# A two-layer mLSTM and band-attention trunk: pieces of x, the gates' products and their selection in the first phase

## The chip, the cores and the metric

The kernel runs on one core of a Trainium2 chip. The metric is the device time of one execution in microseconds; several executions are timed and the median is given. Engines are named as in the profile: PE (matrix products) and PEld (its weight loads), DVE (vector), ACT (scalar, with function tables), POOL, and SP, which issues most transfers.

## The reference

`x` is 512 tokens by 2048 features, batch 1, float32. Two layers follow, each with a pre-norm modulated by a conditioning vector `c`, a mixer, and a gated, normalised residual. The first layer is an mLSTM with 8 heads, the second a chunked band attention. The change touches the start of the first layer:

```python
sc = jax.nn.silu(c)
mod = sc @ ada_w[l] + ada_b[l]                 # shift, scale, gate
h = rmsnorm(x, g_pre[l]) * (1 + scale) + shift
proj = h @ w_in                                # 2048 x (2*2048 + 3*4096 + 16)
qk = silu(causal_conv(proj[..., :A_V0]))       # queries, keys
v, o, z = ...                                  # 4096 columns each
gates = proj[..., A_G0:] + gate_b              # the last 16 columns
li = gates[..., :8]                            # input gates of 8 heads
lf = log_sigmoid(gates[..., 8:])               # forget gates of 8 heads
ht = mlstm_chunkwise(q, k, v, li, lf)          # then head norm, sigmoid(o), silu(z), w_out
```

## The kernel before

Activations lie transposed: 16 depth tiles of 128 features by 512 tokens. Float32 precision is made from three products of a high and a low part (`mm3`): each weight piece is split by ACT into a high part (`wh`) and by DVE into the rest (`wl`), and so is each depth tile of the normalised input (`h1[k]`, parts 0 and 1). A product of 128 by 128 weights with 512 tokens is one PE instruction.

**The start.** SP issues the loads in a fixed order (`pin` keeps program order): `c`, then `x` in four pieces of 4 depth tiles (`xt`, L538), the column constants, small constants (`kcs`, with the identity and a selection matrix `sel`), the first adaLN rows, the first weight pieces. ACT squares a piece two tiles at a time (L583), DVE adds the squares (L586, L588), and PE sums over features for each piece (`token_sums`, tile `ps_x`), with wake-up products (`awake`, tile `ps_idle`) after each but the first. ACT takes the root (L594), DVE the reciprocal (L597), PE spreads it over partitions (`ps_rb`), and the first depth tile of the input is made (L481 to L484, tiles `h1t` and `h`).

**The first phase.** A depth tile of the input is ready only when DVE has summed its two adaLN columns, shift and scale, each a pass over 2048 values per partition (L512). So head 0's columns, and some of head 1's, are computed depth tile by depth tile. `LEAD` lists the columns whose sums stay in PSUM for the whole phase (tile `ps_lead`, five banks of pool `psP` and one of `psA`): each depth tile multiplies all of them at once. `LATER` lists the other columns. They are worked off block by block (`BLOCKS`: depth tiles 0-1, 2-5, 6-11, 12-15) while the next block's depth tiles are being prepared; each column's block sum goes through a `psA` bank (tile `ps_l`) and is copied (L683) or added by DVE (L685) into SBUF. `first_steps()` deals these steps out between the depth tiles. Weight pieces are read in the order of `stream()`, and SP's loads of adaLN rows are interleaved at fixed pieces (`fetch_first`).

**The gates.** After the phase the 2048 by 16 gate weights are loaded (`graw`, L697) and split into a high and a low part side by side (`gw`, 32 columns). In head 0 `gates()` multiplies them with both parts of all 16 depth tiles (tile `ps_g`, 32 products), copies the 32 rows to SBUF (L707), and folds them with two small products by `sel` into `ps_li` and `ps_f` (8 rows each). A chain on ACT and DVE (L714 to L732) makes the log gates, their running sums and maxima.

The scheduler orders each engine's queue by priority, which is program order unless `high_priority` raises it; a queue, once ordered, is worked off in order. PSUM has eight banks, five in `psP` and three in `psA`. `background()` fetches the remaining adaLN rows through POOL and lets DVE sum them.

Of the kernel before, what the change touches and what calls it, by code (L numbers as in the profile page):

```python
# [9 lines left out]
F32 = mybir.dt.float32  # L10
# [5 lines left out]
P = 128  # L16
D = 2048
S = 512
# [13 lines left out]
REL = 257  # L32
EXTW = 640
AHEAD = 300
RAW_BUFS = 3

PAIRS = [(0, 1), (2, 3)]
BLOCKS = [(0, 2), (2, 6), (6, 12), (12, 16)]
LEAD = [0, P, V0 // 2, V0 // 2 + P, O0, O0 + P]
LATER = [O0 + 2 * P, O0 + 3 * P] + [Z0 + i * P for i in range(4)]  # L40
LATER += [DK, DK + P, V0 // 2 + DK, V0 // 2 + DK + P]


# [19 lines left out]
def first_steps():  # L63


    out, left = [], []
    for k0, k1 in BLOCKS:
        n = k1 - k0
        for j in range(n):
            out += left[-(-len(left) * j // n) : -(-len(left) * (j + 1) // n)] + [(k0 + j,)]  # L70
        g = 2 if n <= 4 else 1
        left = [(k0, k1, i, g) for i in range(0, len(LATER), g)]
    return out + left


# [82 lines left out]
def hybrid_trunk(ctx, tc, xT, xN, c, adaT, cols, wst, wg, ext, kc, out):  # L158
# [23 lines left out]
    y2c = [dram.tile([P, 2, S], F32, name=f"y2c{i}") for i in range(BH // 2)]  # L182

    cl = const.tile([P, NCOL], F32, name="cl")
    kcs = const.tile([P, 144], F32, name="kcs")
    ones_f = const.tile([P, P], F32, name="ones_f")
    cst = const.tile([P, 4], F32, name="cst")
    mod = const.tile([P, 128], F32, name="mod")
# [7 lines left out]
    nc.vector.memset(cst[:, 1:2], 1.0)  # L196
    eps_c, one_c = cst[:, 0:1], cst[:, 1:2]
    ident = kcs[:, 0:128]
    sel = kcs[:32, 128:144]

    def col(i):
        return cl[:, i : i + 1]
# [330 lines left out]
        pin(nc.sync.dma_start(crow[i], c[i * S : (i + 1) * S].unsqueeze(0)))  # L533
    xt, xq = [], []
    rstd0 = ssum
    for q in range(4):
        t = sp.tile([P, 4, S], F32, name=f"xt{q}")
        pin(nc.sync.dma_start(t, xT[q]))  # L538
        xq.append(t)
        xt += [t[:, j, :] for j in range(4)]  # L540
        if q == 1:
            pin(nc.sync.dma_start(cl, cols))
    pin(nc.sync.dma_start(kcs, kc[:, :144]))
    early = [ada_load(KT, ap_, 2, pin, 2), ada_load(0, sp, 2, pin, 2)]
    steps = first_steps()
    coming = {}

    def fetch_first(n):

        while wpos[0] < min(n, len(steps)):  # L550
            i = wpos[0]
            raw_load(pin)
            if i == 0:
                coming[1] = ada_start(1)
            for k in range(2, KT):
                if i == steps.index((k - 2,)) + 2:
                    coming[k] = ada_start(k)

    fetch_first(3)
# [16 lines left out]

    silu_c(0)
    silu_c(1)
    for q in range(4):
        pair = []  # L580
        for i in range(2):
            sq = xp.tile([P, 2, S], F32, tag="x", name=f"xsq{q}_{i}")
            pin(nc.scalar.activation(sq, xq[q][:, 2 * i : 2 * i + 2, :], AF.Square))  # L583
            if q < 2 and i == 0:
                silu_c(2 + q)
            pin(nc.vector.tensor_tensor(sq[:, 0, :], sq[:, 0, :], sq[:, 1, :], op=ALU.add))  # L586
            pair.append(sq[:, 0, :])
        pin(nc.vector.tensor_tensor(pair[0], pair[0], pair[1], op=ALU.add))  # L588
        token_sums(pair[0], q == 0, q == 3)
        if q:  # L590
            awake(256 if q < 3 else 128)
# [12 lines left out]
    pin(nc.scalar.copy(rstd0, psr))  # L604
    ada_sum(*early[1], pin)
    h1 = []
    lead = [newp(f"ps_lead{i}") for i in range(5)] + [newa("ps_lead5")]
    oz = [acp.tile([P, S], F32, tag="so", name=f"oz0_{i}", bufs=6) for i in range(6)]
    oz += [q1p.tile([P, S], F32, tag="oz", name=f"oz0_{i}", bufs=2) for i in range(6, 8)]
    qk1 = [q1p.tile([P, S], F32, tag="q1", name=f"q1_{i}", bufs=4) for i in range(4)]  # L610
    later = oz[2:] + qk1
    split_n = [1]

    def split_first(n):
# [24 lines left out]
    def background(n):  # L639
# [4 lines left out]
        while pending and len(loaded) < 3:  # L644
            p, bufs = (bp, 1) if len(pending) % 3 == 1 else (ap_, 2)
            loaded.append(ada_load(pending.pop(0), p, bufs, pin, queue=nc.gpsimd))

    due = []
    for n, step in enumerate(steps):
        if n > len(steps) - 6:  # L650
            background(2 if n % 2 else 0)
        if n:
            split_first(n + 2)
        if due:
            column_sums(due.pop())
        if len(step) == 1:
            [k] = step
            ht = xp.tile([P, 2, S], F32R, tag="x", name=f"h1_{k}")
            tmp = tp.tile([P, S], F32, tag="t", name=f"h1t_{k}")
            *begun, done = modulated(  # L660
                xt[k], rstd0 if k else psr, amul[:, k : k + 1], mod[:, k : k + 1], ht[:, 0, :], ht[:, 1, :], tmp,
                lambda ins: ins if k else pin(ins),
            )
            if k == 0:
                first[:] = *begun, done
            h1.append(ht)
            proj("a_w_in", h1, lead, 1, k, k + 1, KT - 1, first=0)
            if k + 1 < KT:
                due.append(k + 1)
            if k == 0:  # L670
                column_sums(due.pop())
                fetch_first(4)
            continue
        k0, k1, i0, g = step
        [(hi, lo)] = wpiece("a_w_in")
        for i in range(g):
            ps, acc = newa(f"ps_l{i0 + i}_{k0}"), later[i0 + i]
            for k in range(k0, k1):
                w = slice(((k - k0) * g + i) * P, ((k - k0) * g + i + 1) * P)
                mm3(ps, hi[:, w], lo[:, w], h1[k][:, 0, :], h1[k][:, 1, :], k == k0, k == k1 - 1)  # L680
            with tc.high_priority(AHEAD if k0 else 0):
                if k0 == 0:
                    behind(nc.scalar.copy(acc, ps), parted[1])  # L683
                else:
                    nc.vector.tensor_tensor(acc, acc, ps, op=ALU.add)  # L685
# [5 lines left out]
    ones_r = hp.tile([P, P], F32R, name="ones_r")  # L691
    nc.vector.memset(ones_r.bitcast(F32), 1.0)
    maskd = hp.tile([P, P], F32, name="maskd")
    nc.sync.dma_start(maskd, kc[:, 144:272])
    graw = tp.tile([P, KT, 16], F32, tag="t", name="graw")
    gw = hp.tile([P, KT, 32], F32R, tag="p0", name="gw")
    nc.sync.dma_start(graw, wg)  # L697
    split(gw[:, :, 0:16], gw[:, :, 16:32], graw)


    def gates():
        g_ps = newa("ps_g")
        for k in range(KT):
            for i in range(2):
                mm(g_ps[:32], gw[:, k, :], h1[k][:, i, :], k == 0 and i == 0, k == KT - 1 and i == 1)
        g32 = tp.tile([P, S], F32, tag="t", name="g32")
        nc.scalar.copy(g32[:32], g_ps[:32])  # L707
        ps_i, ps_f = newa("ps_li"), newa("ps_f")
        mm(ps_i[:8], sel[:, 0:8], g32[:32], True, True)
        mm(ps_f[:8], sel[:, 8:16], g32[:32], True, True)  # L710
        f, u, w = (hp.tile([P, S], F32, tag=t, name=f"gate_{t}")[:8] for t in ("nm", "nmd", "p1"))
        e = ssum[:8]
        gbi, gbf = cl[:8, GB : GB + 1], cl[:8, GB + 1 : GB + 2]
        nc.scalar.activation(f, ps_f[:8], AF.Identity, bias=gbf)  # L714
        nc.scalar.activation(e, f, AF.Abs)
        nc.scalar.activation(e, e, AF.Exp, scale=-1.0)
        nc.vector.tensor_scalar(u, e, 1.0, None, op0=ALU.add)
        nc.vector.scalar_tensor_tensor(e, u, -1.0, e, op0=ALU.add, op1=ALU.subtract)
        nc.vector.reciprocal(w, u)
        nc.vector.tensor_tensor(e, e, w, op=ALU.mult)  # L720
        nc.scalar.activation(u, u, AF.Ln)
        nc.vector.tensor_tensor(u, u, e, op=ALU.subtract)
        nc.vector.scalar_tensor_tensor(f, f, 0.0, u, op0=ALU.min, op1=ALU.subtract)
        on = tp.tile([P, S], F32, tag="t", name="gate_one")[:8]
        nc.vector.memset(on, 1.0)
        nc.vector.tensor_tensor_scan(u, on, f, 0.0, ALU.mult, ALU.add)
        nc.vector.scalar_tensor_tensor(e, ps_i[:8], gbi, u, op0=ALU.add, op1=ALU.subtract)
        nc.vector.tensor_tensor_scan(w, e, e, 0.0, ALU.max, ALU.max)
        nc.vector.tensor_scalar(on, w, -1.0, None, op0=ALU.mult)
        nc.sync.dma_start(gsc[0], on)  # L730
        nc.vector.tensor_tensor(w, u, w, op=ALU.add)
        nc.scalar.activation(w, w, AF.Exp, scale=-1.0)  # L732
        nc.sync.dma_start(gsc[1], w)
        pt = newa("ps_at")
        for j in range(4):
            nc.tensor.transpose(pt[:, j * 8 : j * 8 + 8], e[:, j * P : (j + 1) * P], ident[:8, :8])
        nc.vector.tensor_copy(aT.rearrange("p a b -> p (a b)"), pt[:, :32])
# [88 lines left out]
    for h in range(NH):  # L826
# [24 lines left out]
        if h == 0:  # L851
            background(2)
            gates()
            for i in range(4):
                nc.scalar.activation(so[i], lead[4 + i] if i < 2 else so[i], AF.Sigmoid)
        nm = hp.tile([P, S], F32, tag="nm", name=f"nm{h}")
        em = ssum
        nmd = hp.tile([P, 4, P], F32, tag="nmd", name=f"nmd{h}")
# [566 lines left out]
def layouts(x, c, ada_w, ada_b, g_pre, g_post, a_w_in, a_conv_w, a_conv_b, a_gate_b, a_g_head,  # L1425
# [3 lines left out]
    def cc(v):  # L1429
        return np.asarray(v).reshape(-1, P).T  # L1430

    xT = np.ascontiguousarray(x[0].T.reshape(4, 4, P, S).transpose(0, 2, 1, 3))
    xN = np.ascontiguousarray(x[0].reshape(4, P, D))
    adaT = np.concatenate([ada_w[0].T, ada_w[1].T, kv_ada_w.T], 0).reshape(128, P, D)
    gb = np.zeros((P, 2), f)
# [14 lines left out]
    rel = b_rel[0]  # L1450
    u = np.clip(384 + (P - 1) - np.arange(EXTW), -128, 128) + 128
    ext = np.ascontiguousarray(rel[:, u])
    kc = np.zeros((P, 272), f)
    kc[:, :128] = np.eye(P)
    i = np.arange(P)
    kc[:32, 128:144] = np.tile(np.eye(16), (2, 1))
    kc[:, 144:272] = np.where(i[None, :] >= i[:, None], 0.0, NEG)
    return {
        "xT": xT, "xN": xN, "c": np.ascontiguousarray(c[0]), "adaT": np.ascontiguousarray(adaT), "cols": np.ascontiguousarray(cols),
        "wst": wst, "wg": wg, "ext": ext, "kc": kc,  # L1460
# [17 lines left out]
```

## Time and profile before

| | |
|---|---|
| median of 3 runs | 2753.21 us (2752.81 to 2754.87) |
| the profiled execution | 2749.57 us, span 2747.5 us |
| PE busy | 2725.0 us (99%) |
| DVE, ACT busy | 2322.9 us (85%), 1436.2 us (52%) |
| DMA | 527.26 MB, mean 192 GB/s |
| granted PE clock | 0.999 |

The span runs from the first to the last instruction; the execution's own time has 2.07 us more around it. "Idle before, releaser" in a row is the time in which the engine stood still ahead of the instruction and what ended it. Rows of a stage give busy time and, in brackets, the number of instructions that touch the stage. DVE shares its busy time unevenly: it is almost full in the first 140 us.

### The profile page before, as it was taken

The page shows a single profiled execution, that of the slowest core. Times are in us where ns is not written, and L with a number is a line of the kernel's source. Part 1 is how long each engine was busy: PE and PEld are TensorE (multiplying, and loading weights), DVE is VectorE, ACT ScalarE, POOL GpSimd, SP SyncE. Part 2 cuts the span into 40 slices and gives each one's busy share as a digit, 9 for nine tenths or more (in the row PEclk, how much of TensorE's full clock was granted, in tenths as well). Part 3 has the DMA queues.
Part 4 walks back from the last instruction along what each step waited for, and adds up shares of the span by engine and source line. Part 5 has one row for each costly group of instructions (what it writes and reads, how often), then busy time and mean ns, then how long its engine had stood idle before and what let it go on. Part 6 is the DMA issues. An engine that isn't in the chain of part 4 may idle for free.

```text
span 2747.5 us, 45189 instructions
## 1 busy us (share of the span) xinstructions
PE 2725.0 (99%) x17554; PEld 2485.9 (90%) x17554; DVE 2322.9 (85%) x3768; ACT 1436.2 (52%) x2046; POOL 30.5 (1%) x61
## 2 busy tenths in 40 slices
PE   8999999999999999999999999999999999999998
PEld 6887888899999999999998888888998999999887
DVE  8988989989999898998988677467995798899666
ACT  4243533556556555565646344568444566666523
POOL 0000010000000000000000000000000000000000
PEclk9999999999999999999999999999999999999999
DMA  9777697333333333333337788788645544444697
GB/s 368 289 263 266 253 375 291 107 99 125 108 116 109 102 125 101 116 110 101 125 101 259 260 294 306 232 282 272 214 146 192 169 123 130 127 125 126 213 305 254
DMA packets 170913, 527.26 MB, mean 192 GB/s; under 512 B 18325, under 2 KB 34229, under 8 KB 158921
## 3 DMA queue, kind: packets, MB, share of 16 engines
q1 hardware_dynamic: 162490, 464.61, 50.6%
q0 software_dynamic: 8208, 59.77, 5.7%
q8 instruction: 137, 2.24, 0.3%
q14 instruction: 78, 0.64, 0.1%
HBM read 490.69 MB, written 38.85 MB: 193 GB/s over the span
## 4 chain that ended last, share of the span: by engine, by line
PE 88%; issue 6%; DVE 3%; DMA 2%; POOL 1%; ACT 1%; SPq 0%; DVEq 0%; POOLq 0%; ACTq 0%
PE ps_y L281 19%; PE ps_azo L281 5%; PE ps_czo L281 5%; PE ps_dzo L281 5%; PE ps_kv L281 5%; PE ps_az L281 3%; PE ps_cz L281 3%; PE ps_dz L281 3%; PE ps_l L281 3%; PE ps_bzo L281 3%; PE ps_czq L281 2%; PE ps_cv L281 2%; PE ps_azq L281 2%; PE ps_dzq L281 2%; PE ps_dv L281 2%
## 5 line engine op out<-in xcount | busy, mean ns | idle before, releaser
L214 ACT CAST wh<-wr 128x1024 fp32r<-128x1024 f32 (+1 forms) x560 | 579.5, 1037 | 534.6 <-PE ps_y L281 205.7
L214 DVE TENSOR_TENSOR wl<-wr,wh 128x1024 fp32r<-128x1024 f32 (+1 forms) x560 | 672.4, 1204 | 183.7 <-ACT wh L214 182.7
L281 PE MATMUL ps_y<-wh,y 128*128 128x512 f32 x1536 | 476.2, 390 | 0.0
L214 ACT CAST wsh<-ws 128x768 fp32r<-128x768 f32 (+1 forms) x272 | 222.5, 818 | 426.8 <-issue 124.8
L281 PEld LDWEIGHTS ps_y<-wh,y 128*128 128x128 f32 x1536 | 288.2, 188 | 59.9 <-ACT sqy L1011 0.2
L214 DVE TENSOR_TENSOR wsl<-ws,wsh 128x768 fp32r<-128x768 f32 (+1 forms) x272 | 253.7, 933 | 91.6 <-ACT wsh L214 88.7
L281 PE MATMUL ps_y<-wl,y 128*128 128x512 f32 x768 | 299.1, 389 | 0.0
L512 DVE CUSTOM_DVE_ANT_0 ada<-ada,scB,cl 128x2048 f32<-128x2048 f32 (+1 forms) x89 | 205.9, 2321 | 14.1 <-DMA ada<-in_adaT 13.8
L253 DVE TENSOR_TENSOR ws<-wr 128x512 f32<-128x512 f32 (+1 forms) x272 | 181.0, 670 | 1.9 <-DMA wr<-in_wst 1.8
L281 PEld LDWEIGHTS ps_y<-wl,y 128*128 128x128 f32 x768 | 144.3, 188 | 29.9 <-DVE wl L214 0.4
L281 PE MATMUL ps_kv<-wh,hkv 128*128 128x512 f32 x512 | 159.5, 390 | 0.0
L281 PE MATMUL ps_v<-wh,h 128*128 128x512 f32 x384 | 120.3, 390 | 0.0
L281 PEld LDWEIGHTS ps_kv<-wh,hkv 128*128 128x128 f32 x512 | 96.1, 188 | 19.9
L255 DVE TENSOR_TENSOR ws<-wr 128x256 f32<-128x256 f32 (+1 forms) x272 | 110.9, 412 | 2.8
L254 DVE TENSOR_TENSOR wr<-ws,wr 128x256 f32<-128x256 f32 (+1 forms) x272 | 110.4, 411 | 1.9
L281 PE MATMUL ps_kv<-wl,hkv 128*128 128x512 f32 x256 | 100.0, 391 | 0.8 <-DVE wl L214 0.8
L281 PE MATMUL ps_l<-h,wh 128*128 128x512 f32 x320 | 98.5, 390 | 0.0
L281 PEld LDWEIGHTS ps_v<-wh,h 128*128 128x128 f32 x384 | 71.9, 188 | 14.7
L281 PE MATMUL ps_azo<-h,wh 128*128 128x256 f32 (+1 forms) x404 | 82.1, 294 | 0.0
L281 PE MATMUL ps_v<-wl,h 128*128 128x512 f32 x192 | 74.9, 390 | 0.0
L281 PEld LDWEIGHTS ps_l<-h,wh 128*128 128x128 f32 x320 | 59.9, 188 | 12.8 <-ACT wh L214 0.3
L281 PE MATMUL ps_dzo<-h,wh 128*128 128x256 f32 x364 | 69.6, 283 | 0.0
(443 smaller groups left out, 7231.8 us busy)
## 6 DMA issues: line engine op xcount, KB each, us to landing
wr<-in_wst SPq DMA_DIRECT2D x530, 512.0 KB, 4.0
ada<-in_adaT POOLq DMA_DIRECT2D x57, 1024.0 KB, 7.0
ada<-in_adaT SPq DMA_DIRECT2D x30, 1024.0 KB, 8.1
adq<-in_adaT SPq DMA_DIRECT2D x92, 256.0 KB, 4.5
ada<-in_adaT SPq DMA_DIRECT2D x36, 512.0 KB, 5.7
xt<-nsc SPq DMA_DIRECT2D x48, 256.0 KB, 3.6
wr<-in_wst SPq DMA_DIRECT2D x26, 384.0 KB, 8.0
yr<-ysc SPq DMA_DIRECT2D x28, 256.0 KB, 5.5
```

Source lines behind the costliest of these rows:

```text
L214: ins = nc.scalar.copy(hi, src), nc.vector.tensor_tensor(lo, src, hi.bitcast(F32), op=ALU.subtract)
L253: nc.vector.tensor_tensor(t[:, : 2 * w], r[:, w : 3 * w], r[:, : 2 * w], op=ALU.subtract)
L254: nc.vector.tensor_tensor(r[:, w : 2 * w], t[:, w : 2 * w], r[:, :w], op=ALU.add)
L255: nc.vector.tensor_tensor(t[:, 2 * w :], r[:, 3 * w :], r[:, w : 2 * w], op=ALU.subtract)
L281: product[0] = nc.tensor.matmul(ps, a, b, start=start, stop=stop)
L512: pin(nc.vector.tensor_tensor_reduce(c, c, (sc or scB)[:, j * w : (j + 1) * w], 1.0, mod[:, i : i + 1] if j else col(CB + i), ALU.mult, AL ...
```

## The change

Three edits. `x` comes in pieces of 4, 4, 6 and 2 depth tiles instead of four of 4; the squares' adds follow the size of the piece. The sixth lead column tile moves to the later ones (five lead, eleven later), and its `psA` bank is taken by the gates' sum: the gate weights are loaded early, split when depth tile 2 is ready, and each depth tile's two gate products are issued right behind its lead products (depth tiles 0 and 1 together with 2). The two selecting products become one, whose 40 rows hold the input gates at 0 to 7 and the forget gates at 32 to 39.

```diff
+CHUNKS = [4, 4, 6, 2]
-LEAD = [0, P, V0 // 2, V0 // 2 + P, O0, O0 + P]
-LATER = [O0 + 2 * P, O0 + 3 * P] + [Z0 + i * P for i in range(4)]
+LEAD = [0, P, V0 // 2, V0 // 2 + P, O0]
+LATER = [O0 + i * P for i in range(1, 4)] + [Z0 + i * P for i in range(4)]
 LATER += [DK, DK + P, V0 // 2 + DK, V0 // 2 + DK + P]
@@ first_steps
-        left = [(k0, k1, i, g) for i in range(0, len(LATER), g)]
+        left = [(k0, k1, i, min(g, len(LATER) - i)) for i in range(0, len(LATER), g)]
@@ loads
-    for q in range(4):
-        t = sp.tile([P, 4, S], F32, name=f"xt{q}")
-        pin(nc.sync.dma_start(t, xT[q]))
+    for q, n in enumerate(CHUNKS):
+        t = sp.tile([P, n, S], F32, name=f"xt{q}")
+        pin(nc.sync.dma_start(t, xT[P * len(xt) : P * (len(xt) + n)].rearrange("(p j) t -> p j t", j=n)))
...
+    graw = sp.tile([P, KT, 16], F32, name="graw")
+    gw = sp.tile([P, KT, 32], F32R, name="gw")
@@ fetch_first
                 if i == steps.index((k - 2,)) + 2:
+                    if k == 2:
+                        pin(nc.sync.dma_start(graw, wg))
                     coming[k] = ada_start(k)
@@ squares
-    for q in range(4):
+    for q, n in enumerate(CHUNKS):
         pair = []
-        for i in range(2):
+        for i in range(n // 2):
...
-        pin(nc.vector.tensor_tensor(pair[0], pair[0], pair[1], op=ALU.add))
+            if i:
+                pin(nc.vector.tensor_tensor(pair[0], pair[0], pair[i], op=ALU.add))
@@ first phase
-    lead = [newp(f"ps_lead{i}") for i in range(5)] + [newa("ps_lead5")]
+    lead = [newp(f"ps_lead{i}") for i in range(5)]
+    g_ps = newa("ps_g")
...
-    later = oz[2:] + qk1
+    later = oz[1:] + qk1
...
+    gated = []
+
+    def gate_products():
+
+        while len(gated) < len(h1):
+            k = len(gated)
+            for i in range(2):
+                mm(g_ps[:32], gw[:, k, :], h1[k][:, i, :], k == 0 and i == 0, k == KT - 1 and i == 1)
+            gated.append(k)
...
             proj("a_w_in", h1, lead, 1, k, k + 1, KT - 1, first=0)
+            if k == 2:
+                split(gw[:, :, 0:16], gw[:, :, 16:32], graw, done, begun[1])
+            if k > 1:
+                gate_products()
@@ gates
-        g_ps = newa("ps_g")
-        for k in range(KT):
-            for i in range(2):
-                mm(g_ps[:32], gw[:, k, :], h1[k][:, i, :], k == 0 and i == 0, k == KT - 1 and i == 1)
         g32 = tp.tile([P, S], F32, tag="t", name="g32")
         nc.scalar.copy(g32[:32], g_ps[:32])
-        ps_i, ps_f = newa("ps_li"), newa("ps_f")
-        mm(ps_i[:8], sel[:, 0:8], g32[:32], True, True)
-        mm(ps_f[:8], sel[:, 8:16], g32[:32], True, True)
+        ps = newa("ps_if")
+        mm(ps[:40], sel, g32[:32], True, True)
...
-        nc.scalar.activation(f, ps_f[:8], AF.Identity, bias=gbf)
+        nc.scalar.activation(f, ps[32:40], AF.Identity, bias=gbf)
...
-        nc.vector.scalar_tensor_tensor(e, ps_i[:8], gbi, u, op0=ALU.add, op1=ALU.subtract)
+        nc.vector.scalar_tensor_tensor(e, ps[:8], gbi, u, op0=ALU.add, op1=ALU.subtract)
@@ head 0
-                nc.scalar.activation(so[i], lead[4 + i] if i < 2 else so[i], AF.Sigmoid)
+                nc.scalar.activation(so[i], so[i] if i else lead[4], AF.Sigmoid)
```

The host's layout of `x` and of the small constants follows.

More of the change, by code (lines that the diff above doesn't have):

```diff
@@ L184, in hybrid_trunk @@
     cl = const.tile([P, NCOL], F32, name="cl")
-    kcs = const.tile([P, 144], F32, name="kcs")
+    kcs = const.tile([P, 168], F32, name="kcs")
     ones_f = const.tile([P, P], F32, name="ones_f")
@@ L198, in hybrid_trunk @@
     ident = kcs[:, 0:128]
-    sel = kcs[:32, 128:144]
+    sel = kcs[:32, 128:168]
     def col(i):
@@ L535, in hybrid_trunk @@
     rstd0 = ssum
-    for q in range(4):
-        t = sp.tile([P, 4, S], F32, name=f"xt{q}")
-        pin(nc.sync.dma_start(t, xT[q]))
+    for q, n in enumerate(CHUNKS):
+        t = sp.tile([P, n, S], F32, name=f"xt{q}")
+        pin(nc.sync.dma_start(t, xT[P * len(xt) : P * (len(xt) + n)].rearrange("(p j) t -> p j t", j=n)))
         xq.append(t)
-        xt += [t[:, j, :] for j in range(4)]
+        xt += [t[:, j, :] for j in range(n)]
         if q == 1:
             pin(nc.sync.dma_start(cl, cols))
-    pin(nc.sync.dma_start(kcs, kc[:, :144]))
+    pin(nc.sync.dma_start(kcs, kc[:, :168]))
     early = [ada_load(KT, ap_, 2, pin, 2), ada_load(0, sp, 2, pin, 2)]
+    graw = sp.tile([P, KT, 16], F32, name="graw")
+    gw = sp.tile([P, KT, 32], F32R, name="gw")
     steps = first_steps()
@@ L693, in hybrid_trunk @@
     maskd = hp.tile([P, P], F32, name="maskd")
[L694 to L698, printed above, removed]
+    nc.sync.dma_start(maskd, kc[:, 168:296])
     def gates():
-        g_ps = newa("ps_g")
-        for k in range(KT):
-            for i in range(2):
-                mm(g_ps[:32], gw[:, k, :], h1[k][:, i, :], k == 0 and i == 0, k == KT - 1 and i == 1)
         g32 = tp.tile([P, S], F32, tag="t", name="g32")
         nc.scalar.copy(g32[:32], g_ps[:32])
-        ps_i, ps_f = newa("ps_li"), newa("ps_f")
-        mm(ps_i[:8], sel[:, 0:8], g32[:32], True, True)
-        mm(ps_f[:8], sel[:, 8:16], g32[:32], True, True)
+        ps = newa("ps_if")
+        mm(ps[:40], sel, g32[:32], True, True)
         f, u, w = (hp.tile([P, S], F32, tag=t, name=f"gate_{t}")[:8] for t in ("nm", "nmd", "p1"))
@@ L1430, in cc @@
         return np.asarray(v).reshape(-1, P).T
-    xT = np.ascontiguousarray(x[0].T.reshape(4, 4, P, S).transpose(0, 2, 1, 3))
+    xT = x[0].T.reshape(KT, P, S)
+    ends = np.cumsum([0] + CHUNKS)
+    xT = np.concatenate([xT[a:b].transpose(1, 0, 2).reshape(-1, S) for a, b in zip(ends, ends[1:])])
     xN = np.ascontiguousarray(x[0].reshape(4, P, D))
@@ L1452, in layouts @@
     ext = np.ascontiguousarray(rel[:, u])
-    kc = np.zeros((P, 272), f)
+    kc = np.zeros((P, 296), f)
     kc[:, :128] = np.eye(P)
     i = np.arange(P)
-    kc[:32, 128:144] = np.tile(np.eye(16), (2, 1))
-    kc[:, 144:272] = np.where(i[None, :] >= i[:, None], 0.0, NEG)
+    kc[:32, 128:136], kc[:32, 160:168] = np.split(np.tile(np.eye(16), (2, 1)), 2, 1)
+    kc[:, 168:296] = np.where(i[None, :] >= i[:, None], 0.0, NEG)
     return {
```

## The prediction

> **What bounds the kernel now.** I read the page first, then the matrix engine's waits in the first 210 us, then the busy time of the stages around them, then the start instruction by instruction. The page gives the engines' shares of the 2747.5 us span.
>
> ```profile
> PE 2725.0 (99%) x17554; PEld 2485.9 (90%) x17554; DVE 2322.9 (85%) x3768; ACT 1436.2 (52%) x2046; POOL 30.5 (1%) x61
> ```
>
> PE is nearly always busy, so an edit can win only where PE waits or does needless work. The changed code lies in the first 240 us. PE's waits there, between the first lead product and the end of the first phase, with total, times and longest, are four groups:
>
> ```profile
> PE ps_lead L281 <- ACT h L483: 2.3, 3, 1.5
> PE ps_l L281 <- DVE wl L214: 0.9, 2, 0.6
> PE ps_lead L281 <- DVE h L484: 0.8, 2, 0.5
> PE ps_lead L281 <- ACT wh L214: 0.7, 1, 0.7
> ```
>
> That is 4.7 us, and everything before the first lead product is the second reserve. The stages, with busy time and (in brackets) instructions of PE, PEld, DVE, ACT and POOL, then granted clock, DMA share and GB/s:
>
> ```profile
> 25.80:134.70 108.90, 104.17 (x445) 82.17 (x443) 106.94 (x127) 33.99 (x48) 0.00 (x0) 1.00 0.84 326
> 134.70:216.00 81.30, 81.28 (x358) 64.64 (x359) 66.23 (x81) 32.96 (x41) 3.82 (x7) 1.00 0.70 259
> 181.00:208.40 27.40, 27.40 (x123) 22.68 (x122) 26.71 (x33) 15.92 (x20) 2.11 (x4) 1.00 0.65 225
> ...
> 134.72 0.50 PE L281 MATMUL ps_l<-h,wl 128*128 128x512 f32 x1 [0.61 <-DVE wl L214]
> ```
>
> Up to 134.7 us DVE works 106.94 of 108.90 us: it paces the stage, and PE catches up with it from time to time. The last catch is the fourth row, from the timeline. After it PE is full (358 products in 81.3 us, 0.227 us each) and drags its backlog to the end of the phase. So the end of the phase is the time of that last catch plus PE's work still to do.
>
> **The start: pieces of 4, 4, 6 and 2.** These rows carry it (start, length, engine, line):
>
> ```profile
> 12.51 2.00 ACT L583 ACTIVATE xsq<-xt 128x1024 f32<-128x1024 f32 x2 [0.70 <-DMA xt<-in_xT]
> 15.12 2.00 ACT L583 ACTIVATE xsq<-xt 128x1024 f32<-128x1024 f32 x2 [0.60 <-DMA xt<-in_xT]
> 17.15 0.69 DVE L586 TENSOR_TENSOR xsq<-xsq 128x512 f32<-128x512 f32 x1 [0.26 <-ACT xsq L583]
> 17.88 0.69 DVE L588 TENSOR_TENSOR xsq<-xsq,xsq 128x512 f32<-128x512 f32 x1
> 17.74 0.55 PEld L281 LDWEIGHTS ps_idle<-scB,ones_f 128*128 128x128 f32 x2
> 18.68 1.78 PEld L281 LDWEIGHTS ps_x<-ones_f,xsq 128*128 128x128 f32 x8 [0.39 <-issue]
> 20.59 0.26 ACT L594 ACTIVATE rc<-ps_x,cst 128x4 f32<-128x4 f32 x1 [2.17 <-PE ps_x L281]
> 21.14 0.22 DVE L518 SCALAR_TENSOR_TENSOR amul<-mod,cst,cl 128x1 f32<-128x1 f32 x1
> 21.27 0.17 DVE L597 RECIPROCAL rc<-rc 128x4 f32<-128x4 f32 x1
> 25.85 0.19 PEld L281 LDWEIGHTS ps_lead<-h,wh 128*128 128x128 f32 x1 [0.44 <-ACT h L483]
> ```
>
> The third and fourth pieces land at 12.51 and 15.12, so a 4-tile piece takes 2.61 us. The last byte still lands at 15.12, but a third piece of 6 tiles lands 1.30 us later than one of 4, at 13.81. ACT then has four squares in a row, 0.97 us apart (two take 2.00): the third ends at 16.8, the fourth at 17.8. DVE does five adds for that piece, where a piece of 4 takes three, about 0.6 us apart and 0.73 where one needs the other: the sum of the 6-tile piece starts at 17.9, just where the last sum of all starts now, and the add of the 2-tile piece follows at 18.5. So at 18.68, where PE now does the token sums of the last piece, it does those of the third. Then come the wake-up products (0.55 us of loads; the products overlap the next loads) and only then eight more for the last piece: from about 21.0 to 22.8, against 20.5 now. ACT's root runs at 22.9 instead of 20.59, and the reciprocal at 23.2 instead of 21.27; it gains back 0.4 because DVE was late there (L518 just before it). Start: **+1.9 us**. If the wake-up products stand behind the token sums it is +1.4; if they overlap with nothing, +2.3.
>
> Of that, part is swallowed by the next wait on a transfer (the stage's row as above, and the wait):
>
> ```profile
> 20.00:40.00 20.00, 18.23 (x70) 13.64 (x71) 18.86 (x24) 6.28 (x10) 0.00 (x0) 1.00 1.02 415
> ...
> 34.96 0.69 DVE L214 TENSOR_TENSOR wl<-wr,wh 128x512 fp32r<-128x512 f32 x1 [0.72 <-ACT wh L214]
> ```
>
> The piece that ACT casts there comes from a queue that is full (DMA share 1.02 at 415 GB/s from 20 to 40 us), and its bytes hardly change: two lead pieces lose 64 KB each, the gates' weights add 128 KB. It lands when it landed, so DVE loses this 0.72 us of idling: **-0.7**, from 0 to -0.7.
>
> **DVE's work up to the last catch.** Its kinds, with mean ns of one (the fifth is one sum of an adaLN column), and the gates' split, which moves here from 159.9 us:
>
> ```profile
> L214 DVE TENSOR_TENSOR wl<-wr,wh 128x768 fp32r<-128x768 f32 x15 | 14.2, 951 | 0.0
> L214 DVE TENSOR_TENSOR wl<-wr,wh 128x512 fp32r<-128x512 f32 x5 | 3.4, 687 | 0.7 <-ACT wh L214 0.7
> L255 DVE TENSOR_TENSOR ws<-wr 128x256 f32<-128x256 f32 (+1 forms) x272 | 110.9, 412 | 2.8
> L685 DVE TENSOR_TENSOR q<-q,ps_l 128x512 f32<-128x512 f32 x4 | 2.7, 685 | 0.2
> L512 DVE CUSTOM_DVE_ANT_0 ada<-ada,scB,cl 128x2048 f32<-128x2048 f32 (+1 forms) x89 | 205.9, 2321 | 14.1 <-DMA ada<-in_adaT 13.8
> L214 DVE TENSOR_TENSOR gw<-graw,gw x1: 357/357/357, 159.9 to 159.9; 128x256 fp32r<-128x256 f32 x1
> ```
>
> A lead piece shrinks from 768 to 640 columns: half of the way to 512, -0.13 us, 14 times: -1.85. The eleventh later column adds one piece of 256 columns in the first block (0.41), one of 512 in the second (0.69), one add (0.68), and the gates' split 0.36. Sum **+0.3**; from -0.2, as neighbours overlap by 0.1, to +1.2, if one more third-block piece (0.95) falls before the catch. SP issues the gates' load at the third weight piece; behind it stand the loads for depth tile 2, which wait for buffers anyway, so nothing is charged.
>
> **PE's work on either side of the last catch.** The products of the lead tiles and of the later ones before it:
>
> ```profile
> 25.80:134.70 108.90, 55.93 (x225) 41.48 (x225) 0.00 (x0) 0.00 (x0) 1.00 0.84 326
> ...
> 25.80:134.70 108.90, 52.57 (x218) 40.69 (x218) 8.20 (x12) 5.72 (x10) 1.00 0.84 326
> ```
>
> The 225 lead products become 188 (five columns of six). Of the 218 later ones, 60 of the first block become 66, 120 of the second 132, and the 38 of the third stay: 236. Twelve depth tiles add 24 gate products. 448 against 443: 5 products more lie before the catch and 5 fewer after it: **-1.1 us**. Over the whole phase nothing is saved, since the 32 gate products only change place:
>
> ```profile
> L281 PE MATMUL ps_g<-h,gw x32: 390/396/398, 208.5 to 215.7; 128*32 128x512 f32 x32
> 216.97 1.02 PE L281 MATMUL ps_li<-g,kcs 32*8 32x512 f32 x2
> 217.83 1.02 PE L281 MATMUL ps_f<-g,kcs 32*8 32x512 f32 x2
> 218.78 0.50 PE L281 MATMUL ps_v<-wl,h 128*128 128x512 f32 x1
> ```
>
> A gate product has a stream of 512 like any other, so it costs a full slot. The first six wait for DVE's split of the gates' weights in PE's queue, behind the lead products of depth tile 2; the later pieces queue behind them. If DVE puts the split behind one adaLN sum (2.3 us), PE idles up to that long, but the catches that come later (4.7 us of waits less the 1.5 and 0.7 of the first two) swallow it; charged at nothing, at most +2.3.
>
> **The selection.** From 216.97 to 218.78 four passes take 1.8 us; two go: **-0.9 us**, on PE's path, since PE is full around it. The ACT and DVE steps behind it stay as they are.
>
> Sum: +1.9 - 0.7 + 0.3 - 1.1 - 0.9 = **-0.5 us**. The profiled execution took 2749.57 us (2.07 us outside its span), so it would take 2749.1; the median of the three runs, 2753.21, lies 3.6 above that execution, and the same step gives **2752.7 us**. With the bounds of the terms the case runs from about 2750.5 to 2756.5. A measurement of this kernel can tell about 0.2% from no change, 5.5 us: this is no change.
>
> **Rival 1, faster: the gate products fill PE's waits.** For it: they need no new data, and they stand just where PE waits for the next depth tile. Against it: DVE's 98% says the catches come when DVE is ready, and the lead products given up are the same filler. If the scheduler places them so that all 4.7 us of waits go, and the start is not later, the gain is 4.7 + 0.9 = 5.6: **2747.6 us**. With the later start it would be 2749.5, no change. Chance of the full gain, or of more than I see: 0.17.
>
> **Rival 2, slower: the gates' chain lands in the phase's tail, and PSUM runs short there.** Now the chain runs behind the tail, beside the value products. With the gates summed by the last depth tile it can start near 181 us, where ACT and DVE do convolutions and the third pool's banks turn over.
>
> ```profile
> 202.12 0.68 DVE L685 TENSOR_TENSOR q<-q,ps_l 128x512 f32<-128x512 f32 x1
> ...
> 204.99 0.68 DVE L685 TENSOR_TENSOR q<-q,ps_l 128x512 f32<-128x512 f32 x1
> 206.00 0.69 DVE L685 TENSOR_TENSOR q<-q,ps_l 128x512 f32<-128x512 f32 x1 [0.33 <-PE ps_l L281]
> ...
> 223.26 3.33 DVE L719 RECIPROCAL gate_p<-gate_nmd 8x512 f32<-8x512 f32 x1
> ...
> 219.59 0.63 ACT L715 ACTIVATE ssum<-gate_nm 8x512 f32<-8x512 f32 x1
> 220.24 1.28 ACT L716 ACT_TABLE_LOAD   x1
> 221.54 0.63 ACT L716 ACTIVATE ssum<-ssum 8x512 f32<-8x512 f32 x1
> ```
>
> A tail tile is 12 products, 2.72 us. The add at 206.00 starts as its tile ends; the two before ended near 203.2 and 200.5, so their adds were 1.8 and 1.6 us late. While the chain holds one of three banks, PE stalls from a lateness of 2.72 - 0.69 = 2.03 us on. DVE is 97% busy from 181 to 208; the reciprocal alone (3.33) costs 3.33 - 2.03 = 1.3 us, and a pair of background sums (L512) with no add between (4.6) 2.6. One of the first and two of the second are 6.5 us: **2759.2 us**. Against it: the adds have high priority, and g's copy can free its bank at once. ACT is a second way to the same stall: the chain has three table loads, 1.30 us each by the rows (the activation at 221.54 follows at once), 3.9 us in a stretch where ACT works 15.92 of 27.40.
>
> The Trainium skill's page "ScalarE: Activation LUTs", section "What ACT_TABLE_LOAD costs", puts a switch of table at about 2.66 us, because of a drain beside the load itself; by it the three would take 8.0 us. The trace disagrees: no drain is seen around the load at 220.24.
>
> Chance of the stalls, or of another wait of that size: 0.17.
>
> **Rival 3: the products are not spread.** PE's order is set by priority, and the products could queue up behind all lead products. Then the -1.1 goes and the rest stands: +0.6, **2753.8 us**, still no change. Chance 0.10; my own forecast has 0.56.
>
> **How the numbers follow.** Faster 0.17 (rival 1), slower 0.17 (rival 2), within 0.2% 0.56 + 0.10 = 0.66. The range takes in the forecast's bounds, rival 3, and the near end of rivals 1 and 2: 2747.6 to 2758.0.
>
> **What would show it.** Right: the reciprocal of the root near 23.2 us and the first lead product near 27.8; PE's waits up to 140 us about as large as now; one selection of two passes; the value products of the first head starting within 2 us of 216. Wrong: a first lead product before 26.5 (the start step), waits on DVE's gate split above 2.3 us, PE's waits in 30 to 140 us below 2 us (rival 1), or new waits of PE on L685 between 181 and 212 us (rival 2). A time below 2747.7 or above 2758.7 makes the forecast wrong.

## The result: slower, and not in the first phase

The changed kernel takes 2780.85 us (median of 5 runs, 2779.14 to 2783.19) against 2753.21 (5 runs, 2752.21 to 2754.87): 1.0096 of the time before, 95% interval 1.0085 to 1.0108. That is 27.6 us more, where 0.5 less was forecast.

The first rows are the page's, for the kernel before (its shares of the span stand above) and the changed one: the shares, then the costliest products of 512 tokens (busy time, mean ns of one).

```profile
L281 PE MATMUL ps_y<-wh,y 128*128 128x512 f32 x1536 | 476.2, 390 | 0.0
```

```profile
PE 2752.6 (99%) x17552; PEld 2484.8 (89%) x17552; DVE 2330.0 (84%) x3775; ACT 1440.3 (52%) x2053; POOL 30.6 (1%) x61
...
L282 PE MATMUL ps_y<-wh,y 128*128 128x512 f32 x1536 | 487.3, 397 | 0.0
```

PE issues two products fewer and is busy 27.6 us longer. The rows on `ps_y` belong to the output projections, more than 1200 us behind the last edited line; the same 1536 products take 397 ns instead of 390. The windows say the same in a stage where PE waits for nothing, 160 to 180 us, before and after:

```profile
160.00:180.00 20.00, 20.00 (x90) 16.55 (x89) 8.78 (x11) 6.36 (x8) 0.00 (x0) 1.00 0.47 167
```

```profile
160.00:180.00 20.00, 20.00 (x87) 15.75 (x87) 9.72 (x13) 4.70 (x6) 0.00 (x0) 1.00 0.54 205
```

PE is full in both, its clock is 1.00 in both, and yet 87 products fit where 90 did. Take the time from the start of each 512-wide product of the trace to the start of the next product, called its pitch below (gaps above 300 ns left out). The mean is 227.4 ns before, 88% of them 226 or 227, and 234.0 after, nearly all between 230 and 238. The 256-wide ones (gaps above 150 left out) go from 119.9 to 119.4. By counts, 5350 x 6.6 ns - 11320 x 0.5 ns is about 30 us, enough for the whole loss, and it lies all over the kernel.

The operands' start addresses, as the built programs hold them, are a difference that reaches so far. `kcs` grew from 144 to 168 columns, 96 bytes per partition, and everything stacked behind it on that side of SBUF moved by 96: the activations (`h1`, `hkv`, `y`) start at 224 modulo 256 before and at 64 after. The split weights `wh` and `wl` are stacked from the other end, and stay at 224. Either side can be the moving operand, the one that streams past what PEld has loaded; it stands first behind the arrow. In `ps_y<-wh,y` it is `wh` and `y` is loaded; in `ps_lead<-h,wh` it is `h`.

### The profile page after: what moved, and what is told of

The parts are those of the page before. It is cut to its first block, busy times and chain, and to the rows that moved or that the text cites. A ratio compares the mean times of both kernels' runs of the same rounds, so it can differ in the third digit from the quotient of the medians.

```text
span 2777.4 us, 45216 instructions
## 1 busy us (share of the span) xinstructions
PE 2752.6 (99%) x17552; PEld 2484.8 (89%) x17552; DVE 2330.0 (84%) x3775; ACT 1440.3 (52%) x2053; POOL 30.6 (1%) x61
## 4 chain that ended last, share of the span: by engine, by line
PE 93%; DVE 3%; ACT 1%; issue 1%; DMA 1%; SPq 0%; DVEq 0%; POOL 0%; ACTq 0%; POOLq 0%
PE ps_y L282 19%; PE ps_kv L282 6%; PE ps_azo L282 5%; PE ps_dzo L282 5%; PE ps_czo L282 5%; PE ps_l L282 4%; PE ps_v L282 4%; PE ps_dz L282 3%; PE ps_cz L282 3%; PE ps_az L282 3%; PE ps_bzo L282 3%; PE ps_o L282 3%; PE ps_azq L282 2%; PE ps_dzq L282 2%; PE ps_czq L282 2%; PE ps_s L282 2%
## 5 line engine op out<-in xcount | busy, mean ns | idle before, releaser
L215 ACT CAST wh<-wr 128x1024 fp32r<-128x1024 f32 (+3 forms) x564 | 580.7, 1031 | 585.2 <-PE ps_y L282 258.4
L215 DVE TENSOR_TENSOR wl<-wr,wh 128x1024 fp32r<-128x1024 f32 (+3 forms) x564 | 674.7, 1198 | 205.6 <-ACT wh L215 204.0
L282 PE MATMUL ps_y<-wh,y 128*128 128x512 f32 x1536 | 487.3, 397 | 0.0
L282 PEld LDWEIGHTS ps_kv<-wh,hkv 128*128 128x128 f32 x512 | 96.4, 188 | 23.2
L256 DVE TENSOR_TENSOR ws<-wr 128x256 f32<-128x256 f32 (+1 forms) x272 | 111.5, 415 | 2.8
L282 PE MATMUL ps_l<-h,wh 128*128 128x512 f32 x352 | 110.0, 396 | 0.0
L282 PEld LDWEIGHTS ps_l<-h,wh 128*128 128x128 f32 x352 | 66.1, 188 | 16.9
L282 PE MATMUL ps_dzo<-h1s,wh 128*128 128x256 f32 x364 | 69.6, 283 | 0.0
```

Of the source, the lines that this page charges most:

```text
L215: ins = nc.scalar.copy(hi, src), nc.vector.tensor_tensor(lo, src, hi.bitcast(F32), op=ALU.subtract)
L256: nc.vector.tensor_tensor(t[:, 2 * w :], r[:, 3 * w :], r[:, w : 2 * w], op=ALU.subtract)
L282: product[0] = nc.tensor.matmul(ps, a, b, start=start, stop=stop)
```

## The experiments

**Layout or phase.** Theory L: the start addresses alone do it. Rival P: something that the edits leave behind in the first phase.

```diff
-    kcs = const.tile([P, 144], F32, name="kcs")              # e1: kernel before
+    kcs = const.tile([P, 168], F32, name="kcs")[:, :144]     # e3: 160, e4: 152, e6: 208
-    kcs = const.tile([P, 168], F32, name="kcs")              # e2: changed kernel
+    kcs = const.tile([P, 176], F32, name="kcs")[:, :168]     # e5, e7, e11: 208
```

> The kernel before, with nothing changed but the width reserved for the constant tile kcs: 168 columns instead of 144, as in the changed kernel, so that every tile behind it on that side of SBUF lies 96 bytes higher. No instruction, transfer or order is different. Theory L (layout): the start addresses alone turn the 512-wide products from 227 ns apart into about 234, and the time goes to 2776 to 2784 us, though none of the three edits of the first phase is in it. Rival P (phase): the loss comes from something the edits do in the first phase that lasts (PE's clock after the dip at 36 us, the order of its queue); then this kernel stays at 2753 +- 3 us and its products at 227 ns.

Measured (e1): 2779.63 us, ratio 1.0086 (1.0070 to 1.0103). Not one edit of the first phase is in this kernel. Its page and its window:

```profile
PE 2756.9 (99%) x17554; PEld 2485.4 (89%) x17554; DVE 2326.9 (84%) x3768; ACT 1436.5 (52%) x2046; POOL 30.6 (1%) x61
...
L281 PE MATMUL ps_y<-wh,y 128*128 128x512 f32 x1536 | 487.3, 397 | 0.0
...
160.00:180.00 20.00, 20.00 (x87) 16.13 (x86) 7.77 (x11) 3.78 (x5) 0.00 (x0) 1.00 0.50 183
```

The `ps_y` row is that of the changed kernel to the last digit, and 233.9 ns is the mean pitch. Rival P falls: 96 bytes of unused constant tile cost 25 us of the 27.6.

> The changed kernel, with 176 columns reserved for kcs instead of 168, so that the tiles behind it lie 128 bytes higher than before the change instead of 96. All three edits are in it. Theory L: its 512-wide products are again 227 ns apart, and the time is what the prediction's own terms make it, 2750 to 2757 us. Rival P: the products stay near 234 ns and the time at 2776 to 2784 us.

Measured (e2): 2768.71 us, ratio 1.0050 (1.0035 to 1.0065), 232.5 and 118.8 ns. Neither theory's number: the loss is halved, so it is the layout, but 128 bytes aren't a period.

> The kernel before with 160 columns reserved for kcs: the tiles behind it lie 64 bytes higher. Theory L says that start addresses matter, not by which rule. If they count modulo 64 bytes this is as fast as before (2753 +- 3 us); if modulo 128, it is slower, like the shift of 96 (2765 to 2785 us). Rival P: 2753 +- 3 us.

Measured (e3): 2761.12 us, 1.0023 (1.0014 to 1.0033); 232.2 and 118.5 ns. Not as fast as before, so the period isn't 64; below the range given for a period of 128 too; and part of what the 512-wide products lose the 256-wide ones win back.

> The kernel before with 152 columns reserved for kcs: the tiles behind it lie 32 bytes higher, as a shift of 96 would if only the address modulo 64 bytes counts. Theory L modulo 64: the same as a shift of 96, 2776 to 2784 us with products near 234 ns. Theory L modulo 128: a time of its own, above 2753. Rival P: 2753 +- 3 us.

Measured (e4): 2763.99 us, 1.0034 (1.0022 to 1.0046); 233.3 and 118.3 ns. Not the time of the shift of 96 either. When the pitches of these traces are sorted by the distance between the address of the moving operand and that of the operand loaded for it, modulo 256, one group stands out: with 0 throughout, as in the kernel before, 227.2 ns for 512-wide products; with 64, 229.4; with every other multiple of 32, 232 to 234. For 256-wide products 0 is among the slow ones (119.9), and so is 96 (119.9 as well). Hence theory L256. Not every product follows it: some 160 512-wide products of two activations (`ps_s<-k,q`, `ps_n<-p,v`, `ps_o<-pt,vv`) keep distance 0 in every layout, and are about 232 ns apart before the change and 233 after it.

> The kernel before with 208 columns reserved for kcs: every tile behind it 256 bytes higher, no edit of the change. Theory L256: 2753 +- 3 us, 512-wide products at 227 ns. Rival (any shift off the first layout costs): above 2757 us.

Measured (e6): 2754.68 us, 1.0006 (0.9997 to 1.0015); 227.4 and 119.9 ns. A shift of 256 costs nothing that can be measured.

> The changed kernel with 208 columns reserved for kcs, so that the tiles behind it lie 256 bytes higher than before the change. Theory L256: what counts is the distance of a product's moving operand from the weights that are loaded beside it, modulo 256 bytes; the two lie on opposite sides of SBUF, at a distance of 0 before the change, and 0 again here. The 512-wide products go back to 227 ns, and the time is that of the three edits alone: 2751 to 2757 us (from the shift of 128: 2768.7, less 5350 products x 5.1 ns, plus 11300 of the 256-wide x 1.1 ns, is 2754). Rival L128 (only the address modulo 128, or a longer period, counts): 2765 us or more, products at 232 ns or more.

Measured (e5): 2758.55 us, 1.0014 (1.0005 to 1.0023); 227.3 and 119.9 ns. The pitch is back, and rival L128 falls; the time is 1.5 us above the expected range.

```profile
PE 2728.1 (99%) x17552; PEld 2490.4 (90%) x17552; DVE 2327.0 (84%) x3775; ACT 1439.3 (52%) x2053; POOL 30.5 (1%) x61
...
L282 PE MATMUL ps_y<-wh,y 128*128 128x512 f32 x1536 | 476.5, 390 | 0.0
```

With the distance at 0 again the row is back at 390. All three edits together cost 0.05 to 0.23%, 1.4 to 6.3 us: this is the part of the loss that the layout doesn't make (3.9 us by the medians of e5 and e6, which are shifted alike).

**Moving the weights instead.** If the distance counts, the 256-wide products should gain when it isn't 0, while the 512-wide ones keep theirs.

```diff
+            at = 16 if groups else 0        # e9: 32, e10: 8; e12: 4 for all pieces
-            hi = wp.tile([P, 1024], F32R, tag="hi", name=f"wh{i}")[:, :n]
+            hi = wp.tile([P, 1088], F32R, tag="hi", name=f"wh{i}")[:, at : at + n]
 ...                                         # lo, and sh and sl likewise
```

> The kernel before with only this edit: the split weights that feed 256-wide products start 64 bytes further into their buffers (buffers 256 bytes longer, so that the others stay where they were). The 512-wide products keep distance 0; nearly all of the 11439 256-wide ones go from distance 0 to 64 or 192 bytes. Theory L256: the 256-wide products go from 119.9 ns to about 117.7, as those with these distances did in the shifted kernels, the 512-wide stay at 227; the time falls by 11160 x 2.2 ns = 24.5 us to 2727 to 2735 us. Rival (the distances only went with something else in the shifted kernels): 2753 +- 3 us.

Measured (e8): 2723.89 us, ratio 0.9894 (0.9879 to 0.9910), faster than both kernels by over 1%, and 3 us below the expected range. The 512-wide products are 227.5 ns apart, the 256-wide 116.6 instead of 119.9, more than the shifted kernels had shown. Before, and here:

```profile
L281 PE MATMUL ps_dzo<-h,wh 128*128 128x256 f32 x364 | 69.6, 283 | 0.0
```

```profile
PE 2697.3 (99%) x17554; PEld 2453.0 (90%) x17554; DVE 2319.8 (85%) x3768; ACT 1437.1 (53%) x2046; POOL 30.5 (1%) x61
...
L282 PE MATMUL ps_y<-wh,y 128*128 128x512 f32 x1536 | 476.8, 390 | 0.6 <-ACT sqy L1012 0.6
...
L282 PE MATMUL ps_dzo<-h,wh 128*128 128x256 f32 x364 | 68.7, 281 | 0.0
```

PE does the same 17554 instructions in 27.7 us less; no instruction was taken out.

> As the kernel before with the weights of 256-wide products moved by 64 bytes, but by 128. Theory L256: the distance alone sets the pitch, so nearly all 256-wide products now have 128 bytes. In the changed kernel shifted by 128 those with that distance were 118.5 ns apart, beside others at 0; on their own they should be between 116.6 (as at 64) and 118.5, and the time 2724 to 2742 us. If only a multiple of 128 counts as near (period 128), they stay at 119.9 and the time at 2754.

Measured (e9): 2744.38 us, 0.9961 (0.9947 to 0.9975); 256-wide 118.7 ns. Just outside the expected range, at its dear end, but not the 119.9 of a period of 128.

> The same with 32 bytes (distances 32 and 224 for the 256-wide products). They were 117.7 to 118.0 ns apart in the shifted kernels, beside others at 0. Theory L256 with steps of 32 bytes: 116.5 to 118 ns, 2722 to 2738 us. If the two sides are compared by 64-byte lines only, it is as with 0: 119.9 ns and 2754 us.

Measured (e10): 2738.50 us, 0.9942 (0.9928 to 0.9955); 256-wide 118.2 ns, a little above the range. So 64 is the best of the three, and lines of 64 bytes aren't the rule.

> The kernel before with all split weights, those of the 512-wide products too, moved by 16 bytes: distances of 16 and 240 bytes instead of 0 for both widths. Theory L256 with steps of 32 bytes: 16 counts as 0 (or as 32 where it crosses a step); as 0, both widths keep 227.4 and 119.9 ns and the time stays at 2754 us. If the distance counts more finely, the 256-wide products gain (116.5 to 118 ns, 20 to 37 us) and the 512-wide lose (229 to 234 ns, 10 to 37 us): 2735 to 2765 us with both pitches moved.

Measured (e12): 2757.66 us, 1.0009 (0.9999 to 1.0018); 512-wide 231.7 ns, 256-wide 118.4. Sixteen bytes count: the 512-wide products with distance 16 and those with 240 both lie between 231 and 232 ns, so neither counts as 0, and steps of 32 aren't the rule.

**Distance, or the address itself.** The runs above moved one side at a time.

```diff
+    kcs = const.tile([P, 160], F32, name="kcs")[:, :144]
+            hi = wp.tile([P, 1088], F32R, tag="hi", name=f"wh{i}")[:, 16 : 16 + n]      # lo too
```

> The kernel before with both sides moved by 64 bytes: 160 columns reserved for kcs (as in the shift of 64) and the split weights hi and lo 64 bytes further into their buffers, for all products. The 512-wide products keep distance 0, but both operands start at 32 modulo 256 instead of 224. Theory D (the distance between the operands counts): the 512-wide products are 227 ns apart, 5 ns less than with the left side moved alone, and the time is 2737 to 2757 us (part of the 256-wide products have distances of 64 and 192 and may gain). Theory A (each start address counts for itself, and 224 happened to be the good one): the 512-wide products are 229 to 234 ns apart and the time is 2757 to 2785 us.

Measured (e13): 2734.07 us, ratio 0.9917 (0.9898 to 0.9936), 2.9 us below the range of theory D; 512-wide 227.3 ns with both operands at 32 modulo 256, where moving the activations' side alone (e3) made it 232.2. For 512-wide products theory D holds and theory A falls. The gain comes from the 256-wide ones, 118.0 ns apart, part of which now have distances of 64 and 192. Its row:

```profile
L281 PE MATMUL ps_y<-wh,y 128*128 128x512 f32 x1536 | 476.3, 390 | 0.0
```

**What is left of the change itself.** Two runs take single edits back at the layout of the shift of 256.

```diff
-CHUNKS = [4, 4, 6, 2]                       # e7
+CHUNKS = [4, 4, 4, 4]
-            if k > 1:                       # e11
+            if k == KT - 1:
                 gate_products()
```

> As the changed kernel shifted by 256 bytes, with x again in four pieces of 4 depth tiles. The prediction's start step says that the pieces 4, 4, 6, 2 put the first lead product 1.9 us later and that about 0.7 of it is swallowed: here the first lead product starts near 25.9 us instead of 27.9, and the time is 1.2 to 3.5 us shorter than that of the pieces 4, 4, 6, 2 at the same layout (the upper end if PE's clock also stays up at 36 us, where it fell to half for 3.4 us). Rival: the delay is swallowed by DVE's later waits, and the two times agree within 1 us.

Measured (e7): 2757.93 us, 1.0014 (1.0005 to 1.0023), against 2758.55 and 1.0014 with 4, 4, 6, 2: the rival's case, though intervals of this width can't exclude 1.2 us, the near end of what was expected. The lead products and the first value products (the end of the phase), with 4, 4, 6, 2 and then with 4, 4, 4, 4; the last pair of numbers ahead of the semicolon is first and last start:

```profile
L282 PE MATMUL ps_lead<-h,wh x160: 387/389/819, 28.1 to 186.1; 128*128 128x512 f32 x160
L282 PE MATMUL ps_v<-wh,h x384: 388/389/628, 218.1 to 519.0; 128*128 128x512 f32 x192
```

```profile
L282 PE MATMUL ps_lead<-h,wh x160: 387/389/1356, 25.9 to 186.5; 128*128 128x512 f32 x160
L282 PE MATMUL ps_v<-wh,h x384: 388/389/628, 218.4 to 517.8; 128*128 128x512 f32 x192
...
40.00:50.00 10.00, 7.27 (x21) 4.83 (x20) 9.93 (x14) 4.37 (x8) 0.00 (x0) 0.70 1.00 384
...
53.14 0.59 ACT L704 COPY oz<-ps_l 128x512 f32<-128x512 f32 x1 [3.03 <-PE ps_l L282]
54.28 0.69 DVE L215 TENSOR_TENSOR wl<-wr,wh 128x512 fp32r<-128x512 f32 x1 [2.65 <-ACT wh L215]
```

The lead products start 2.2 us earlier, and the phase ends no earlier. The last three rows show where the lead goes: PE's clock, which fell near 36 us with 4, 4, 6, 2, falls here between 40 and 50 us, ACT waits 3.03 us for PE's sum before a copy, and DVE 2.65 us for the cast behind that copy. Up to 125 us DVE waits 3.4 us for ACT's casts here and 0.7 us with 4, 4, 6, 2, so PE's last wait for DVE in the phase ends at 124.85 us here and at 124.50 there.

> The changed kernel shifted by 256 bytes, with all 32 gate products behind the lead products of the last depth tile instead of two behind each. Five lead columns, pieces of x and the one selection stay. The prediction's step on PE's work says that spreading them puts 24 products ahead of the last catch of DVE and is worth 1.1 us for the whole change, so without it the time is 1 to 5 us longer than with the spread products (the upper end if the five lead columns alone leave PE idle long enough for its clock to fall). Rival: the wait for the gates' split is what the spread costs, PE's waits then swallow nothing, and the time here is 1 to 2 us shorter.

Measured (e11): 2758.39 us, 1.0017 (1.0008 to 1.0026): no difference from the spread products that can be measured, neither the 1 to 5 us longer nor the rival's 1 to 2 us shorter. In the profiled execution the phase ends 3.7 us later than with the products spread (218.1):

```profile
PE ps_lead L282 <- ACT h L484: 4.9, 3, 2.3
PE ps_lead L282 <- DVE h L485: 1.5, 2, 0.9
...
L282 PE MATMUL ps_v<-wh,h x384: 387/389/504, 221.8 to 523.8; 128*128 128x512 f32 x192
```

One execution and the medians disagree, so what the spread is worth stays open between 0 and 4 us.

## Why the prediction was wrong, point by point

**The step that failed is the one price under all others.** "358 products in 81.3 us, 0.227 us each" was taken from the kernel before and used for the changed one, and the products behind the first phase were charged with no change at all. In the changed kernel a 512-wide product takes 0.234 us on average, and the rows far behind the phase show it too. The line that does it, `kcs = const.tile([P, 168], ...)` instead of 144 columns, is in the whole diff, not among the lines shown above, and the prediction doesn't mention it: it adds no step to the first phase. Alone it costs 25 us (e1). No rival had a mechanism that outlasts the first phase; rival 2 had the sign and a fifth of the size, by something that did not occur.

**The start was right.** From the changed kernel's timeline, and PE's waits on the lead products:

```profile
18.65 1.78 PEld L282 LDWEIGHTS ps_x<-ones_f,xsq 128*128 128x128 f32 x8 [2.85 <-ACT xsq L588]
20.94 2.04 PEld L282 LDWEIGHTS ps_x<-ones_f,xsq 128*128 128x128 f32 x8
23.41 0.18 DVE L603 RECIPROCAL rc<-rc 128x4 f32<-128x4 f32 x1 [1.48 <-ACT rc L600]
27.93 0.53 PEld L282 LDWEIGHTS ps_lead<-h,wh 128*128 128x128 f32 x3 [1.03 <-ACT h L484]
...
36.16 0.69 DVE L215 TENSOR_TENSOR wl<-wr,wh 128x512 fp32r<-128x512 f32 x1
...
PE ps_lead L282 <- ACT h L484: 2.6, 2, 2.4
PE ps_lead L282 <- DVE h L485: 1.6, 2, 1.4
```

The third piece's token sums at 18.65, the last piece's at 20.94, the reciprocal at 23.41 and the first lead product at 27.93 stand for the forecast 18.68, 21.0, 23.2 and 27.8. The swallowed 0.7 us is there too: the split that DVE did at 34.96 after 0.72 us of idling now runs at 36.16 without a wait, 1.2 us later. What isn't borne out is that the rest of the delay reaches the end: taking it back (e7) won nothing that can be measured.

**PE's clock had not been considered.** In the changed kernel:

```profile
35.05 1.43 PE L282 MATMUL ps_lead<-h,wh 128*128 128x512 f32 x5 [2.42 <-ACT h L484]
37.08 0.63 PE L282 MATMUL ps_lead<-h,wl 128*128 128x512 f32 x1
37.51 0.63 PE L282 MATMUL ps_lead<-h,wh 128*128 128x512 f32 x1
...
30.00:40.00 10.00, 7.58 (x27) 5.69 (x26) 9.93 (x13) 1.23 (x2) 0.00 (x0) 0.83 0.99 396
```

PE idles for 2.42 us ahead of depth tile 1 (1.46 before), and from 36.66 us on products start 0.43 us apart until 39.97: the granted clock is 0.83 over these 10 us, and about eight products lose 0.2 us each, 1.6 us. Three lead products fewer are 0.7 us less work for PE ahead of depth tile 1, and the first five took 1.43 us where they took 1.71 before. The Trainium skill's page "TensorE: Matmul & The Clock Gate", section "What's actually happening", says that the clock goes to half after an idle window of about 3.4 us; here it fell after 2.42 us of idling. The length of that wait alone doesn't decide it: the kernel of e11 waits 2.3 us at the same place and its clock is 1.00 from 30 to 40 us, while the kernel of e8, whose first phase is the old one, waits 1.8 us there and its clock falls. So it isn't shown that the change makes the clock fall. The row of e8:

```profile
30.00:40.00 10.00, 8.16 (x29) 6.20 (x28) 9.23 (x11) 1.68 (x3) 0.00 (x0) 0.83 1.01 408
```

**The gates' split and the selection were right.** The split stands directly behind the depth tile's own, and PE has no wait on it; the single selection takes 0.98 us up to the next product, where 1.81 were spent.

```profile
46.81 0.74 DVE L485 SCALAR_TENSOR_TENSOR h<-h1t,mod,h 128x512 fp32r<-128x512 f32 x1
47.48 0.42 DVE L215 TENSOR_TENSOR gw<-graw,gw 128x256 fp32r<-128x256 f32 x1
...
221.30 1.05 PE L282 MATMUL ps_if<-g,kcs 32*40 32x512 f32 x2
222.28 0.50 PE L282 MATMUL ps_v<-wh,h 128*128 128x512 f32 x1
```

**Rival 2 did not occur.** PE waits for nothing between 180 and 225 us in the changed kernel, and the gates' chain did not move up: its selection runs at 221.30, behind the tail.

**Rival 3 did not occur either.** The gate products are spread, from 49.8 us on. Rival 1's full gain did not come: 3.9 us of waits on the lead products are left at the layout of the shift of 256.

**The terms together.** At equal pitch the first value product starts at 218.08 us (e5) against 215.95 before, but these aren't the same point of the work: before, four value products run ahead of the selection, in e5 none does. The first rows are from the kernel before, the others from e5; the fifth value product of each is its last row.

```profile
216.42 0.62 PE L281 MATMUL ps_v<-wh,h 128*128 128x512 f32 x2
216.97 1.02 PE L281 MATMUL ps_li<-g,kcs 32*8 32x512 f32 x2
218.78 0.50 PE L281 MATMUL ps_v<-wl,h 128*128 128x512 f32 x1
```

```profile
124.50 0.50 PE L282 MATMUL ps_lead<-h,wh 128*128 128x512 f32 x1 [0.43 <-DVE h L485]
...
217.10 1.05 PE L282 MATMUL ps_if<-g,kcs 32*40 32x512 f32 x2
218.08 0.50 PE L282 MATMUL ps_v<-wh,h 128*128 128x512 f32 x1
...
219.11 0.39 PE L282 MATMUL ps_v<-wl,h 128*128 128x512 f32 x1
```

The fifth value product starts at 219.11 against 218.78: 0.3 us later, where the terms said 0.5 earlier. That is close, and partly luck: the last catch, at which two of the terms were reckoned (+0.3 and -1.1), lies at 124.50 us in e5 and not near 134.7, so neither of them was met as it was meant. The clock's fall near 36 us lies ahead of that catch, and isn't shown to delay the phase's end. So these traces don't show most of the 3.9 us between e5 and e6 in the first phase. Behind it, from 240 to 440 us, PE waits 6.2 us in e5, 3.4 in the kernel before and 5.3 in e6; single executions differ too much to settle where the rest lies. The measured 1.4 to 6.3 us overlap the bounds given (2750.5 to 2756.5 around 2752.7), though the bounds of the single terms add up to 2751.7 to 2757.0.

## What to carry to other kernels

A diff that allocates differently is a diff to every instruction whose operands move: before costing anything else, work out which tiles shift, and compare the pitch of products in a stage far from the edit. For the float32 products of this kernel it pays to choose the distance between the moving operand and the loaded one, modulo 256 bytes, by the width of the product: 0 for 512 columns, and for 256 columns the weights moved by 64, which won 1.1% without touching an instruction's work. To judge an edit, pad the allocation so that these distances stay what they were.

## What was not expected of the hardware

- The pitch of full-clock products depends on where their operands lie. For 512 columns it is 227.4 ns at distance 0 modulo 256, 231.7 at 16, 229.4 at 64, and 232 to 234 at the other distances tried. For 256 columns it is 119.9 at 0, and with the weights moved by 16, 32, 64 and 128 bytes it is 118.4, 118.2, 116.6 and 118.7 (e12, e10, e8, e9; most of these products then have the distance 256 less the move). For 512 columns it is the distance and not the address, since both operands moved by 64 keep 227.3 (e13); for 256 columns this wasn't tried by itself. What in the memory or in PE causes it, the runs don't show.
- The page's granted clock says nothing of it: it is 1.00 in both 160 to 180 us windows.
- PE's clock fell to half after 2.42 us of idling, from about 36.7 to 40.0 us, in the changed kernel, and after 1.8 us in e8, but not after 2.3 us in e11.
